# Laying the high and low halves of the weights among each other, element by element, in a two-layer encoder

## The chip, the cores and the metric

The kernel runs on one core of a Trainium2 chip. Its time is the device time of one execution in microseconds (us); smaller is better. A profiled execution gives the trace that is read here: for each engine (PE for matmuls, PEld for the weight loads of the same engine, DVE, ACT, POOL, and SP, which issues the transfers) the start and length of its instructions.

## The reference

The reference is a trunk of two layers over 256 tokens of width 2048, all in float32. Each layer has two parts, and each part adds its result to the running activations `x`:

```
h = rmsnorm(x, norm_mix[l]) * (1 + sc_a) + sh_a
qa, ka, va, qb, kb, vb, ga, gb = split_cols(h @ w_in[l])
ya = window_attention(qa, ka, va, sink_a[l]) @ w_proj_a[l]
yb = neighbourhood_attention(qb, kb, vb, rel_bias_b[l]) @ w_proj_b[l]
merged = sigmoid(ga) * ya + sigmoid(gb) * yb
x = x + gt_a * (merged @ w_out[l])
h = rmsnorm(x, norm_ffn[l]) * (1 + sc_m) + sh_m
u = depthwise_conv(h @ w_up[l], conv_w[l], conv_b[l])
g, v = split(u)
x = x + gt_m * ((silu(g) * v) @ w_down[l])
```

The shifts, scales and gates (`sh`, `sc`, `gt`) come from a small vector `c` through a matrix `ada_w` of 2048 x 12288 per layer. The weights of one layer are 232 x 16 blocks of 128 x 128 floats, each used once per execution.

## The kernel before

**Split products.** Matmuls run in the type fp32r, which keeps fewer bits than float32. To get float32 accuracy the kernel splits each operand into a high half (the value rounded to fp32r) and a low half (what is left) and adds three products: high weight by high activation, high weight by low activation, low weight by high activation.

**Weights.** The weights come in units of 16 blocks, 1 MB each, in the order in which TensorE uses them. `unit` (line 216) transfers a unit into a tile `w` of the pool `raw` (four buffers) and splits it in two halves of eight blocks. For each of these it takes a tile `hl` (a pool of four buffers, 8 KB per partition each); ACT writes the rounded values into its first 4 KB (line 225, a cast), and DVE subtracts them from the raw values and writes the rest into its last 4 KB (line 226). So there are 928 casts and 928 subtractions of 128 x 1024 elements. Before the change all the high values of eight blocks lie one after another, and then all the low ones.

**Feature stages.** In all products but q, k and v the weight block is the stationary operand: `feature_run` (line 229) loads 128 columns of `hl` and streams an activation tile past them. In the first layer's mixer (`joint`) each block gives three matmuls of 256 columns (lines 239, 240, 241), each with a weight load of its own. Everywhere else a block gives one matmul of 512 columns with the high weights (high and low activation side by side; lines 248 and 253) and one of 256 columns with the low weights (line 250). The first are called wide here, all those of 256 columns narrow. They run in groups of up to eight blocks: for the first half of a sum over 16 blocks the wide ones and then the narrow ones, for the second half the narrow ones and then the wide ones.

**Token stages.** For q, k and v (`tokens`, lines 337 to 339) the roles are swapped: an activation block is stationary, and 512 columns of `hl` (four blocks) stream past it.

**What the stages read.** The streamed activations are the tiles `h` and `merged` (one buffer of the pool `h`), `oA` and `oB` (the outputs of the attention) and `act` (in the shared places `o`, `a`, `b0`, `b1`, `y0` to `y2`). In the built program `hl`, `h` and `merged` begin at a byte offset in the partition that leaves 32 when divided by 128; the places of `act`, `oB` and most of `oA` leave 96.

**Order.** The program's order on each engine comes from the order of the Python statements and a scheduler. The background work (attention heads, the products with `ada_w` on DVE at line 162) is paced by unit. SP issues all transfers of weights; ACT and DVE each run a single queue that holds the splitting of the weights and the evacuation of finished sums.

Of the kernel before, what the change touches and what calls it, by code (L numbers as in the profile page):

```python
# [9 lines left out]
F32 = mybir.dt.float32  # L10
F32R = mybir.dt.float32r
AF = mybir.ActivationFunctionType
ALU = mybir.AluOpType
AX = mybir.AxisListType

P = 128
L = 2
# [16 lines left out]
GATE_A, GATE_B = 4608, 6656  # L34
# [27 lines left out]
ATT = [1.288, 0.4]  # L62
ATT_B = [0.21, 0.21]

ADA_ORDER = [[p * KC + k for k in range(KC) for p in ps] for ps in ((0, 1), (2,), (3, 4), (5,))]
ADA_ORDER = [i for part in ADA_ORDER for i in part]


def block_stream(l):

    seq = []
    for part in K_PARTS[l]:
        for g in QKV_GROUPS:
            for kc in part:
                seq += [("w_in", kc, g // P + j) for j in range(4)]
        for mo in range(KC):
            seq += [("w_in", kc, GATE_A // P + mo) for kc in part]
    for mo in range(KC):
        seq += [("w_proj_a", kc, mo) for kc in range(HA)]
    for mo in range(KC):  # L80
        seq += [("w_in", kc, GATE_B // P + mo) for kc in range(KC)]
    for mo in range(KC):
        seq += [("w_proj_b", kc, mo) for kc in range(HB)]
    for mos in OUT_TURNS:
        seq += [("w_out", kc, mo) for kc in range(KC) for mo in mos]
    for gi, chunks in enumerate(FF_GROUPS):
        cols = [c + h * FC for c in chunks for h in range(2)]
        if gi == 0:
            for kc in range(KC):
                seq += [("w_up", kc, m) for m in cols[:4]]  # L90
            cols = cols[4:]
        for m in cols:
            seq += [("w_up", kc, m) for kc in range(KC)]
        for mos in OUT_TURNS:
            seq += [("w_down", kc, mo) for kc in chunks for mo in mos]
    return seq


UB = 16
NU = len(block_stream(0)) // UB  # L100
NA = len(ADA_ORDER)


@with_exitstack
def encoder(ctx: ExitStack, tc: tile.TileContext, a: dict, out: bass.AP):
    nc = tc.nc
# [4 lines left out]
    hlp = pool("hl", 4)  # L111
# [40 lines left out]
    def ada(l):  # L152
# [5 lines left out]
        mods[l], amods[l] = mod, amod  # L158
        for n, i in enumerate(ADA_ORDER):
            raw = rawp.tile([P, D], F32, name=f"aw{l}_{n}", tag="raw")  # L160
# [54 lines left out]

    def unit(l, u):

        raw = rawp.tile([P, UB * P], F32, name=f"w{l}_{u}", tag="raw")
        nc.sync.dma_start(raw[:], a["ws"][l, u])
        halves = []  # L220
        for j in range(2):
            n = UB * P // 2
            hl = hlp.tile([P, 2, n], F32R, name=f"hl{l}_{u}_{j}", tag="hl")
            r = raw[:, j * n : (j + 1) * n]
            nc.scalar.copy(hl[:, 0], r)  # L225
            nc.vector.tensor_tensor(out=hl[:, 1], in0=r, in1=hl[:, 0].bitcast(F32), op=ALU.subtract)  # L226
            halves.append(hl)
        return halves

    def feature_run(run, joint):  # L230

        wide, narrow = [], []
        for ps, hl, j, act, first, last in run:
            hi, lo = hl[:, 0, j * P : (j + 1) * P], hl[:, 1, j * P : (j + 1) * P]
            out = ps[:].rearrange("p (a s) -> p a s", a=2)
            if joint:
                nc.tensor.matmul(out[:, 0], hi, act[:, 0], start=first, stop=False)  # L239
                nc.tensor.matmul(out[:, 0], hi, act[:, 1], start=False, stop=False)  # L240
                nc.tensor.matmul(out[:, 0], lo, act[:, 0], start=False, stop=last)  # L241
                continue
            wide.append((out, hi, act, first, last))
            narrow.append((out[:, 0], lo, act[:, 0]))
        begins = any(w[3] for w in wide)
        for o, w, act, first, last in wide:
            if begins and not last:
                nc.tensor.matmul(o, w, act, start=first, stop=False)  # L248
        for o, w, act in narrow:
            nc.tensor.matmul(o, w, act, start=False, stop=False)  # L250
        for o, w, act, first, last in wide:
            if last or not begins:
                nc.tensor.matmul(o, w, act, start=False, stop=last)  # L253

    class Stream:
# [16 lines left out]
        def prefetch(self, n):  # L272

            for _ in range(n):
                self.ahead.append(unit(self.l, self.u + len(self.ahead)))
# [13 lines left out]
        def next_block(self):  # L289
            if self.at == UB:  # L290
                if self.ahead:
                    self.halves = self.ahead.popleft()
                else:
                    with self.held():
                        self.halves = unit(self.l, self.u)
                self.u, self.at = self.u + 1, 0
            j = self.at
            self.at += 1
            return self.halves[j // 8], j % 8

        def features(self, acts, evacs, late=None, joint=False):

            pss = [mm.tile([P, 512], F32, name=f"ps{self.l}_{self.u}_{self.at}_{m}", tag="mm") for m in range(len(evacs))]
            run = []
            for i, act in enumerate(acts):
                self.feed(i)
                for ps in pss:
                    hl, j = self.next_block()
                    run.append((ps, hl, j, act, i == 0, i == len(acts) - 1))
                    ends = i == len(acts) - 1 and ps is pss[-1]  # L310
                    if j == 7 or ends or self.near(late, i, acts, ps, pss):
                        feature_run(run, joint)
                        run = []
                        if late and i == len(acts) - LATE - 1:
                            late()
                    if self.at == UB:
                        self.tick()
            for ps, evac in zip(pss, evacs):
                evac(ps)
# [6 lines left out]
        def tokens(self, h, kcs):  # L326

            pss = [mm.tile([P, 512], F32, name=f"ps{self.l}_{self.u}_t{t}", tag="mm") for t in range(2)]
            for kc in kcs:
                self.feed(kc)  # L330
                for _ in range(4):
                    hl, j = self.next_block()
                j -= 3
                hi, lo = hl[:, 0, j * P : (j + 4) * P], hl[:, 1, j * P : (j + 4) * P]
                for t, ps in enumerate(pss):
                    xh, xl = (h[:, kc, i, t * P : (t + 1) * P] for i in range(2))
                    nc.tensor.matmul(ps[:], xh, hi, start=kc == kcs[0], stop=False)  # L337
                    nc.tensor.matmul(ps[:], xh, lo, start=False, stop=False)  # L338
                    nc.tensor.matmul(ps[:], xl, hi, start=False, stop=kc == kcs[-1])  # L339
                if self.at == UB:  # L340
                    self.tick()
            return pss
# [622 lines left out]
```

## Time and profile before

| What | Value |
|---|---|
| Time, median of 3 runs | 2773.54 us (2771.54 to 2773.58) |
| Profiled execution, its own time | 2775.14 us |
| Its span, first to last instruction | 2773.4 us |
| PE busy | 2715.0 us (98%), 15930 matmuls |
| PEld busy | 2398.7 us (86%), 15930 loads |
| DVE busy | 2214.0 us (80%) |
| ACT busy | 1450.3 us (52%) |
| Mean granted TensorE clock | 0.991 |
| DMA, mean | 252 GB/s |

[...] The pace is read from the starts: the time from one matmul's start to the next one's. Where the timeline merges several equal matmuls in one line, the pace is the line's length, less the length of one record, divided by the number of matmuls less one.

### The profile page before, as it was taken

The numbers are of one execution on the slowest core, as the hardware profiler recorded it, in microseconds if no ns is written. First come the engines' busy times: TensorE is split into PE (matmuls) and PEld (weight loads), VectorE is DVE, ScalarE is ACT, GpSimd is POOL, SyncE is SP. The second block draws the span as 40 slices with busy tenths as digits, with TensorE's granted clock in tenths as the row PEclk, the third lists the DMA queues.
The fourth block names the chain that finished last, engine by engine and source line by source line (L and its number), as shares of the span: only waits on it lengthen the run. The fifth ranks groups of instructions, "written<-read, shape, count | busy, mean of one in ns | idle before, by whom it ended". The sixth has DMA issues, their size and how long they took to land.

```text
span 2773.4 us, 39861 instructions
## 1 busy us (share of the span) xinstructions
PE 2715.0 (98%) x15930; PEld 2398.7 (86%) x15930; DVE 2214.0 (80%) x3163; ACT 1450.3 (52%) x2137; POOL 39.3 (1%) x24
## 2 busy tenths in 40 slices
PE   7899999999999999999999999999989999999999
PEld 5788799998888888888878888888878888888888
DVE  6998987897999888789976666768989767766775
ACT  5344684444654455355544567555455535544553
POOL 0000100000000000000000000000000000000000
PEclk9999999999999999999999999999999999999999
DMA  8887588896778766777756666665867655555553
GB/s 314 334 329 264 214 308 329 329 331 231 279 279 328 276 255 245 271 274 286 291 190 238 228 227 233 232 254 199 306 222 287 243 190 187 193 186 194 184 196 137
DMA packets 101852, 699.72 MB, mean 252 GB/s; under 512 B 12705, under 2 KB 15009, under 8 KB 17697
## 3 DMA queue, kind: packets, MB, share of 16 engines
q1 hardware_dynamic: 101666, 697.17, 68.2%
q8 instruction: 125, 2.05, 0.3%
q14 instruction: 61, 0.50, 0.1%
HBM read 695.03 MB, written 2.10 MB: 251 GB/s over the span
## 4 chain that ended last, share of the span: by engine, by line
PE 79%; issue 14%; DVE 4%; POOL 1%; ACT 1%; DMA 0%; POOLq 0%; SPq 0%; ACTq 0%; DVEq 0%
PE ps L253 20%; PE ps L250 18%; PE ps L248 15%; PE ps_t L338 4%; PE ps L240 4%; PE ps L239 4%; PE ps L241 4%; PE ps_t L339 4%; PE ps_t L337 4%; DVE aw L162 1%; DVE hl L226 1%; POOL qrs L390 1%; PE sc L485 1%; PE po L516 1%; ACT hl L225 0%
## 5 line engine op out<-in xcount | busy, mean ns | idle before, releaser
L226 DVE TENSOR_TENSOR hl<-w,hl 128x1024 fp32r<-128x1024 f32 x928 | 1131.3, 1223 | 307.6 <-ACT hl L225 300.8
L225 ACT CAST hl<-w 128x1024 fp32r<-128x1024 f32 x928 | 972.5, 1050 | 756.3 <-PE ps L253 174.5
L162 DVE CUSTOM_DVE_ANT_0 aw<-aw,cact,ab 128x2048 f32<-128x2048 f32 x192 | 450.7, 2347 | 25.5 <-DMA aw<-in_aw 25.1
L250 PEld LDWEIGHTS ps<-h,hl 128*128 128x128 f32 x3328 | 428.0, 191 | 16.9
L250 PE MATMUL ps<-h,hl 128*128 128x256 f32 x3328 | 432.9, 283 | 0.0
L253 PE MATMUL ps<-h,hl 128*128 128x512 f32 x1712 | 428.7, 392 | 0.0
L248 PE MATMUL ps<-h,hl 128*128 128x512 f32 x1616 | 406.4, 394 | 5.5 <-DVE cpad L347 4.5
L248 PEld LDWEIGHTS ps<-h,hl 128*128 128x128 f32 x1616 | 306.3, 190 | 70.8 <-DVE cpad L347 5.4
L253 PEld LDWEIGHTS ps<-h,hl 128*128 128x128 f32 x1712 | 307.9, 189 | 55.0
L346 ACT COPY r<-ps 128x256 f32<-128x256 f32 x240 | 88.9, 372 | 286.0 <-PE ps L253 286.0
L337 PE MATMUL ps_t<-hl,h 128*128 128x512 f32 x576 | 228.1, 401 | 7.5 <-ACT hl L225 7.0
L338 PE MATMUL ps_t<-hl,h 128*128 128x512 f32 x576 | 228.6, 397 | 4.7 <-DVE hl L226 4.7
L339 PE MATMUL ps_t<-hl,h 128*128 128x512 f32 x576 | 227.6, 396 | 0.9 <-DVE h L426 0.9
L826 DVE SCALAR_TENSOR_TENSOR u<-cpad,cw,u 128x256 f32<-128x256 f32 x352 | 168.7, 481 | 7.6 <-ACT u L824 3.2
L241 PE MATMUL ps<-h,hl 128*128 128x256 f32 x512 | 145.9, 285 | 0.0
L239 PE MATMUL ps<-h,hl 128*128 128x256 f32 x512 | 145.3, 284 | 0.0
L240 PE MATMUL ps<-h,hl 128*128 128x256 f32 x512 | 145.0, 283 | 0.0
L786 DVE SCALAR_TENSOR_TENSOR x<-ps,mod,x 128x256 f32<-128x256 f32 x237 | 111.5, 481 | 40.5 <-PE ps L253 30.4
L337 PEld LDWEIGHTS ps_t<-hl,h 128*128 128x128 f32 x576 | 109.8, 191 | 31.1 <-ACT hl L225 7.6
L338 PEld LDWEIGHTS ps_t<-hl,h 128*128 128x128 f32 x576 | 110.0, 191 | 30.8 <-DVE hl L226 8.1
L339 PEld LDWEIGHTS ps_t<-hl,h 128*128 128x128 f32 x576 | 109.9, 191 | 24.3 <-DVE h L426 1.4
L347 DVE TENSOR_TENSOR cpad<-ps,r 128x256 f32<-128x256 f32 x176 | 74.4, 424 | 63.2 <-ACT r L346 63.0
(202 smaller groups left out, 3610.4 us busy)
## 6 DMA issues: line engine op xcount, KB each, us to landing
w<-in_ws SPq DMA_DIRECT2D x464, 1024.0 KB, 4.9
aw<-in_aw SPq DMA_DIRECT2D x192, 1024.0 KB, 4.9
bias<-in_bias SPq DMA_DIRECT2D x16, 256.0 KB, 4.4
x<-in_xT SPq DMA_DIRECT2D x4, 512.0 KB, 5.6
out<-x SPq DMA_DIRECT2D x16, 128.0 KB, 1.8
cw<-in_cw SPq DMA_DIRECT2D x2, 176.0 KB, 4.0
maskA<-in_maskA SPq DMA_DIRECT2D x1, 256.0 KB, 5.3
ab<-in_ab SPq DMA_DIRECT2D x2, 48.0 KB, 7.1
```

The costliest lines, as they stand in the source:

```text
L162: nc.vector.tensor_tensor_reduce(out=raw[:], in0=raw[:], in1=cact[:], scale=1.0, scalar=ab[:, i : i + 1], op0=ALU.mult, op1=ALU.add, accum ...
L225: nc.scalar.copy(hl[:, 0], r)
L226: nc.vector.tensor_tensor(out=hl[:, 1], in0=r, in1=hl[:, 0].bitcast(F32), op=ALU.subtract)
L239: nc.tensor.matmul(out[:, 0], hi, act[:, 0], start=first, stop=False)
L240: nc.tensor.matmul(out[:, 0], hi, act[:, 1], start=False, stop=False)
L241: nc.tensor.matmul(out[:, 0], lo, act[:, 0], start=False, stop=last)
L248: nc.tensor.matmul(o, w, act, start=first, stop=False)
L250: nc.tensor.matmul(o, w, act, start=False, stop=False)
L253: nc.tensor.matmul(o, w, act, start=False, stop=last)
L337: nc.tensor.matmul(ps[:], xh, hi, start=kc == kcs[0], stop=False)
L338: nc.tensor.matmul(ps[:], xh, lo, start=False, stop=False)
L339: nc.tensor.matmul(ps[:], xl, hi, start=False, stop=kc == kcs[-1])
```

## The change

In three of every four units of a layer's weight stream (numbers 0, 1 and 2 of each four), unless the unit holds a block of q, k or v, the high and low values of `hl` no longer lie in two runs of 1024: value 0's high half comes first, then its low half, then value 1's high half, and so on. Tiles, sizes, buffers, transfers, instructions, their order on every engine and all waits are the same; only the addresses that ACT writes, DVE reads and writes and the weight load reads go in steps of two elements there. In the built program 584 of the 928 casts and of the 928 subtractions are of this kind, and the loads of 6144 narrow and 3936 wide matmuls.

```diff
+MESH = [True, True, True, False]
...
-NU = len(block_stream(0)) // UB
+STREAMS = [block_stream(l) for l in range(L)]
+NU = len(STREAMS[0]) // UB
...
     def unit(l, u):
         raw = rawp.tile([P, UB * P], F32, name=f"w{l}_{u}", tag="raw")
         nc.sync.dma_start(raw[:], a["ws"][l, u])
         halves = []
+        mesh = MESH[u % len(MESH)] and not any(m == "w_in" and mo < GATE_A // P for m, _, mo in STREAMS[l][u * UB : (u + 1) * UB])
         for j in range(2):
             n = UB * P // 2
-            hl = hlp.tile([P, 2, n], F32R, name=f"hl{l}_{u}_{j}", tag="hl")
+            hl = hlp.tile([P, 2 * n], F32R, name=f"hl{l}_{u}_{j}", tag="hl")
             r = raw[:, j * n : (j + 1) * n]
-            nc.scalar.copy(hl[:, 0], r)
-            nc.vector.tensor_tensor(out=hl[:, 1], in0=r, in1=hl[:, 0].bitcast(F32), op=ALU.subtract)
-            halves.append(hl)
+            both = hl[:].rearrange("p (n a) -> p a n" if mesh else "p (a n) -> p a n", a=2)
+            nc.scalar.copy(both[:, 0], r)
+            nc.vector.tensor_tensor(out=both[:, 1], in0=r, in1=both[:, 0].bitcast(F32), op=ALU.subtract)
+            halves.append(lambda a, j, n=1, both=both: both[:, a, j * P : (j + n) * P])
         return halves
...
-            hi, lo = hl[:, 0, j * P : (j + 1) * P], hl[:, 1, j * P : (j + 1) * P]
+            hi, lo = hl(0, j), hl(1, j)
...
-                hi, lo = hl[:, 0, j * P : (j + 4) * P], hl[:, 1, j * P : (j + 4) * P]
+                hi, lo = hl(0, j, 4), hl(1, j, 4)
```

## The prediction

> **What bounds the kernel now.** I read the page first: engine shares, then the groups. The columns of a group are line, engine, operation, output and inputs, count, then busy time, mean length of one, idle time before and who ended it.
>
> ```profile
> PE 2715.0 (98%) x15930; PEld 2398.7 (86%) x15930; DVE 2214.0 (80%) x3163; ACT 1450.3 (52%) x2137; POOL 39.3 (1%) x24
> ...
> L226 DVE TENSOR_TENSOR hl<-w,hl 128x1024 fp32r<-128x1024 f32 x928 | 1131.3, 1223 | 307.6 <-ACT hl L225 300.8
> L225 ACT CAST hl<-w 128x1024 fp32r<-128x1024 f32 x928 | 972.5, 1050 | 756.3 <-PE ps L253 174.5
> ```
>
> TensorE hardly ever waits, so the span is its pace; the splitting is beside it, and ACT waits for buffers that TensorE frees. The timeline of PE alone, at four places, shows the pace (start us, length us of the merged line):
>
> ```profile
> 469.79 0.28 PE L239 MATMUL ps<-h,hl 128*128 128x256 f32 x1
> 469.91 0.28 PE L240 MATMUL ps<-h,hl 128*128 128x256 f32 x1
> 470.03 0.28 PE L241 MATMUL ps<-h,hl 128*128 128x256 f32 x1
> ...
> 539.83 0.28 PE L239 MATMUL ps<-oB,hl 128*128 128x256 f32 x1
> 539.94 0.28 PE L240 MATMUL ps<-oB,hl 128*128 128x256 f32 x1
> 540.06 0.28 PE L241 MATMUL ps<-oB,hl 128*128 128x256 f32 x1
> ...
> 1101.15 2.08 PE L250 MATMUL ps<-h,hl 128*128 128x256 f32 x16
> 1103.06 2.00 PE L253 MATMUL ps<-h,hl 128*128 128x512 f32 x8
> ...
> 1119.69 2.02 PE L253 MATMUL ps<-act_y,hl 128*128 128x512 f32 x8
> 1121.55 2.03 PE L248 MATMUL ps<-act_b,hl 128*128 128x512 f32 x8
> ...
> 1900.70 1.07 PE L250 MATMUL ps<-oB,hl 128*128 128x256 f32 x8
> ...
> 2168.80 1.98 PE L248 MATMUL ps<-h,hl 128*128 128x512 f32 x8
> ```
>
> Narrow matmuls that stream `h` start 0.120 us apart: (2.08 - 0.283) / 15, and the first three lines. Those that stream `oB` start (1.07 - 0.276) / 7 = 0.113 us apart. Wide ones on `h` need (1.98 - 0.394) / 7 = 0.227 (line 248) or (2.00 - 0.393) / 7 = 0.230 (line 253), on `act` 0.232 to 0.234. Shape, type, engine queue and neighbours are the same; what differs is where the streamed tile lies against the weights. The view by tile says it in one column (min/median/max ns of one):
>
> ```profile
> L250 PE MATMUL ps<-h,hl x3328: 274/283/415, 674.2 to 2695.1; 128*128 128x256 f32 x196
> L250 PE MATMUL ps<-act_b,hl x384: 276/276/282, 1106.8 to 2549.9; 128*128 128x256 f32 x192
> ```
>
> So a weight load and the matmul that it runs beside disturb each other by an amount that hangs on their addresses, and the change alters the load's addresses. The weight load is the shorter leash for narrow matmuls: transposes with only 128 streamed columns start 0.109 us apart, (0.60 - 0.273) / 3, so 0.109 is what a load of 128 columns needs by itself:
>
> ```profile
> 1700.12 0.60 PE L510 MATMUL tp<-ident,p 128*128 128x128 f32 x4
> 1700.56 1.03 PE L485 MATMUL sc<-packB 128*128 128x256 f32 x4
> ```
>
> **The change, part by part.** (1) Instructions, order, waits, buffers, transfers: none added or moved, on SP, POOL or elsewhere; cost zero, with nothing that needs cover. (2) ACT's cast writes, and DVE's subtraction reads and writes, in steps of two elements, 584 times each. No row here has such a step. Upper bound: half rate. For DVE the part of 1.223 us that grows with length comes from the 256-element L347 at 0.424: (1223 - 424) / 768 = 1.04 ns per element, so at most +1.07 us each, 622 us of DVE work; for ACT, from L346 at 0.372, (1050 - 372) / 768 = 0.88 ns, at most +0.90 us, 528 us. Lower bound: nothing, since one element per step of the engine is already all that 1.04 ns allows; a gain has no row. I take zero, because DVE's rate is the same whether it streams 256, 1024 or 2048 elements (L162: 2347), which says the arithmetic sets it and not the memory. If ACT's bound came true, 1450 + 528 = 1978 us would still fit; DVE's is a rival below.
>
> The Trainium skill, SBUF — State Buffer, on cachelines under "Door 1", says that memory lines are 16 bytes and that two hits on a line keep full rate; every second fp32 is exactly two hits. By that the strided cast, subtraction and load cost nothing by themselves. No run here shows it.
>
> (3) The weight load reads 128 elements over 1024 bytes instead of 512. The streamed operand moves through 1024 bytes in the 0.113 us of a narrow matmul, and the load's 0.109 us now covers 1024 bytes as well: the two walk at the same speed, where before the stream overtook the load. Two walkers at one speed either never meet or, once one has been held up, stop meeting; walkers at different speeds meet again and again. So I expect the disturbed paces to fall to the least disturbed that this trace has, 0.113 narrow and 0.227 wide. Of the 6144 narrow matmuls with changed loads 4352 stream `h` or `merged`: 4352 x (0.120 - 0.1134) = 28.7 us; the other 1792 are within about 0.001 of it: 2 us. Of the 3936 wide ones, 2720 stream `h` or `merged`; half of these are at line 253: 1360 x 0.003 = 4 us; the 1216 on `act`, `oA`, `oB` give 1216 x 0.006 = 7 us. Sum 42 us.
>
> Bounds of (3): downwards, if nothing disturbs any more: narrow 0.109 (L510) and wide 0.216, L485's pace of (1.03 - 0.380) / 3 rounded: with mean paces of 0.118 and 0.230 that is 6144 x 0.009 + 3936 x 0.014 = 110 us less. Upwards, moderate: a load over twice as many bytes collides twice as often; the step from 0.113 to 0.120 is then paid once more, 6144 x 0.0067 = 41 us, and the wide ones pay their excess over 0.227 once more, 4 us at line 253 on `h` and 9 us on `act`: together 54 us more. Upwards, extreme: the load takes a step of two at half rate, 0.218 us, and narrow matmuls follow it: 6144 x 0.100 = 614 us; wide ones at 0.230 still cover it. I take the 42 us, as the rows nearest to it exist in the kernel itself, at the same shapes.
>
> (4) What then comes next: at 42 us less, DVE's 2214 us and the DMA's 252 GB/s mean stay below the new span; in the tightest stretch of the changed part (680 to 800 us, DVE busy 111.76 of 120) a gain of about 2% still fits. I allow 3 us for this and for the first loads after a switch. The profiled execution took 2775.14 us, 1.6 above the median: 2775.1 - 42 + 3 = 2736, against the median 2735.
>
> **The rivals.** *Nothing moves.* The pace might be set by the stream alone, with 0.120 against 0.113 due to where the streamed tile lies and not to the load. Against: the two tiles differ only in offset; for: wide matmuls pay less on `h` and more on `act`, so no tile is simply the bad one. It gives 2774. The Trainium skill says so outright, in TensorE: Matmul & The Clock Gate, the weight-load step under "Step-by-step: what each phase is for": the engine has two independent read ports, and loading the next weights takes nothing from the running matmul. The trace disagrees so far as a row can: 276 against 283 ns for the same form.
>
> *Slower by collisions*, at the weight load: the moderate upper bound above, 54 us, 2828. For it: twice the bytes per load. Against: equal speeds. It decides as soon as narrow matmuls on `h` pass 0.120.
>
> *Slower by DVE*, at line 226: at half rate DVE's load rises by about 0.29 us per us (622 us over the 2093 us that lie behind 400 us and outside the second layer's q, k and v, 1420 to 1700); added to its share by stretch (0.79 at 400 to 500, 0.90, 0.78, 0.93 at 680 to 800, 0.88, 0.81, 0.87, then 0.77, 0.80, 0.72, 0.66) it passes 1 in all but the last, which sums to about 190 us: 2965. It decides where the subtraction passes about 1.47 us (the 8 us free at 680 to 800 over 33 changed tiles).
>
> *Slower by a half-rate load*: 614 us, 3388; it decides from a load longer than the 0.120 us of the narrow pace.
>
> *Undisturbed altogether*: 110 us less, 2664.
>
> **How the numbers follow.** Forecast (paces fall to the best of this trace, 2715 to 2765): 0.52. Undisturbed or nearly (2664 to 2715): 0.08. Nothing: 0.08. Collisions (2780 to 2840): 0.17. DVE: 0.08. Half-rate load: 0.07. So faster by over 0.2% (5.5 us, about what a measurement of this kernel can tell from no change) 0.60, within it 0.08, slower 0.32. The forecast's own range is 2715 to 2765. The whole range takes in half of the undisturbed case, all collisions and the mildest of DVE: 2695 to 2850, leaving out the half-rate load, most of DVE's case and the extreme gain, about 0.17.
>
> **What would show it.** In the profile after: the narrow matmuls of line 250 on `h` at a median of 276 instead of 283 ns and 16 of them in about 1.98 us; unchanged units still at 2.08; the two forms of the cast and the subtraction at the same length, 1.05 and 1.22 us; PE's share still 98%. Wrong, if the subtraction with the step exceeds 1.47 us and PE waits for `hl`, or if narrow matmuls in changed units start more than 0.120 us apart.

## The result, and the profile after

The changed kernel is slower: 2801.98 us against 2772.54 us, a ratio of 1.0106 (95% interval 1.0089 to 1.0124). The page of its profiled execution, whose span is 2799.9 us, 26.5 more than before:

```profile
PE 2740.1 (98%) x15930; PEld 2436.4 (87%) x15930; DVE 2217.7 (79%) x3163; ACT 1494.9 (53%) x2137; POOL 39.3 (1%) x24
...
L233 ACT CAST hl<-w 128x1024 fp32r<-128x1024 f32 x928 | 1023.8, 1105 | 784.3 <-PE ps L261 169.1
L234 DVE TENSOR_TENSOR hl<-w,hl 128x1024 fp32r<-128x1024 f32 x928 | 1131.8, 1223 | 334.9 <-ACT hl L233 330.6
```

(Lines are eight further down from the helpers on: 225, 226, 248, 250, 253 are now 233, 234, 256, 258, 261.) TensorE is as full as before, 98%; so it did not wait for anybody, it got slower. DVE's subtraction did not change by a nanosecond. ACT's cast did: 344 of the 928 are unchanged at 1.050 us, so the 584 others take (1023.8 - 344 x 1.050) / 584 = 1.135 us. PEld, the weight loads, is up by 37.7 us: in the changed units the median load takes 195 ns beside narrow matmuls and 196 beside wide ones, where it took 192 and 188.

The view by source line of the narrow matmuls (min/median/max ns), and the timeline of PE in a stretch that streams `h` and one that streams `oB`:

```profile
L258 PE MATMUL ps<-h,hl x3328: 277/283/416, 675.9 to 2720.8; 128*128 128x256 f32 x196
L258 PE MATMUL ps<-act_b,hl x384: 276/282/288, 1114.9 to 2573.3; 128*128 128x256 f32 x192
```

```profile
1084.74 2.03 PE L256 MATMUL ps<-h,hl 128*128 128x512 f32 x8
1086.61 2.08 PE L258 MATMUL ps<-h,hl 128*128 128x256 f32 x16
1088.52 2.05 PE L261 MATMUL ps<-h,hl 128*128 128x512 f32 x8
...
1907.10 1.12 PE L258 MATMUL ps<-oB,hl 128*128 128x256 f32 x8
```

The narrow matmuls on `h` were to fall from 283 to 276 ns; they stayed, 16 of them still taking 2.08 us. Instead those on `act` and `oB` rose to the slow pace: (1.12 - 0.282) / 7 = 0.120 us against 0.113. And the wide ones on `h` went from 0.227 and 0.230 to (2.03 - 0.400) / 7 = 0.233 at line 256 and (2.05 - 0.396) / 7 = 0.236 at line 261. (Paces are taken from the starts because records overlap: a narrow one on `h` is 0.283 us long, and the next starts after 0.120.)

Adding up the times from each matmul's start to the next one's, by what is streamed (rows where TensorE stood for over 0.4 us left out), gives the whole bill, in us:

| Matmuls | before | after | difference |
|---|---|---|---|
| narrow on `h`, `merged` | 709.7 | 710.8 | +1.1 |
| narrow on `act`, `oA`, `oB` | 286.6 | 296.9 | +10.3 |
| wide on `h`, `merged` | 806.6 | 825.2 | +18.6 |
| wide on `act`, `oA`, `oB` | 380.0 | 377.8 | -2.2 |
| sum | | | +27.8 |

The span grew by 26.5 us; what the table leaves out (long waits, q, k and v, the attention) makes up the difference of about 1 us. What it leaves open is whether the loads read slower or the writes disturb them, and why the load at equal speed did not get out of the stream's way.

### The profile page after: what moved, and what is told of

Its sections match the earlier page's. It is cut to its first block, busy times and chain, and to the rows that moved or that the text cites. A ratio compares the mean times of both kernels' runs of the same rounds, so it can differ in the third digit from the quotient of the medians.

```text
span 2799.9 us, 39861 instructions
## 1 busy us (share of the span) xinstructions
PE 2740.1 (98%) x15930; PEld 2436.4 (87%) x15930; DVE 2217.7 (79%) x3163; ACT 1494.9 (53%) x2137; POOL 39.3 (1%) x24
## 3 DMA queue, kind: packets, MB, share of 16 engines
q8 instruction: 125, 2.05, 0.3%
## 4 chain that ended last, share of the span: by engine, by line
PE 79%; issue 14%; DVE 4%; POOL 1%; ACT 1%; DMA 1%; POOLq 0%; SPq 0%; ACTq 0%; DVEq 0%
PE ps L261 20%; PE ps L258 18%; PE ps L256 16%; PE ps_t L346 4%; PE ps L248 4%; PE ps L249 4%; PE ps L247 4%; PE ps_t L347 4%; PE ps_t L345 4%; DVE aw L166 1%; DVE hl L234 1%; POOL qrs L398 1%; PE po L524 1%; PE sc L493 1%; ACT hl L233 0%
## 5 line engine op out<-in xcount | busy, mean ns | idle before, releaser
L233 ACT CAST hl<-w 128x1024 fp32r<-128x1024 f32 x928 | 1023.8, 1105 | 784.3 <-PE ps L261 169.1
L258 PEld LDWEIGHTS ps<-h,hl 128*128 128x128 f32 x3328 | 430.7, 195 | 17.3
L261 PE MATMUL ps<-h,hl 128*128 128x512 f32 x1712 | 435.4, 396 | 0.0
L256 PE MATMUL ps<-h,hl 128*128 128x512 f32 x1616 | 416.9, 400 | 5.6 <-DVE cpad L355 4.7
L256 PEld LDWEIGHTS ps<-h,hl 128*128 128x128 f32 x1616 | 315.5, 196 | 72.3 <-DVE cpad L355 5.5
L261 PEld LDWEIGHTS ps<-h,hl 128*128 128x128 f32 x1712 | 316.9, 194 | 51.3
```

The costliest lines, as they stand in the source:

```text
L233: nc.scalar.copy(both[:, 0], r)
```

## The experiments

### Only the load reads in steps of two

```diff
-            both = hl[:].rearrange("p (n a) -> p a n" if mesh else "p (a n) -> p a n", a=2)
+            apart, among = hl[:].rearrange("p (a n) -> p a n", a=2), hl[:].rearrange("p (n a) -> p a n", a=2)
+            wr, rd = apart, among if mesh else apart
```

ACT and DVE then write to `wr`, and the matmuls load from `rd`.

> ACT and DVE write the high and low halves apart, as before the change; only the weight load reads in steps of two elements, in the same units as the changed kernel (so it multiplies by wrong weights: high and low values mixed; the work is otherwise the same). Load theory (the step of the load makes the load and the stream beside it disturb each other more): about the whole loss, 2800 us, with wide matmuls on h 0.235 us apart instead of 0.229 and narrow ones on oB and act 0.120 instead of 0.114. Write theory (ACT's cast, which went from 1.05 to 1.14 us in the changed units, or the writes' own disturbance of TensorE's reads): about the time before, 2773 us, with the paces of before.

2801.69 us, ratio 1.0097 (1.0083 to 1.0111): the whole loss. By starts, each of the four groups of the table lies within about 1 us of the changed kernel. The wide matmuls on `h` at line 262 (261 in the changed kernel) have the same busy time as there, 435.4 us, and the cast is back at its old length:

```profile
L234 ACT CAST hl<-w 128x1024 fp32r<-128x1024 f32 x928 | 973.9, 1051 | 794.4 <-issue 180.9 <-PE ps L262 178.4 <-PE ps L259 156.5
L262 PE MATMUL ps<-h,hl 128*128 128x512 f32 x1712 | 435.4, 396 | 0.0
```

### Only the writes go in steps of two

```diff
-            wr, rd = apart, among if mesh else apart
+            wr, rd = among if mesh else apart, apart
```

> The reverse: ACT and DVE write the halves among each other in the changed units, the weight load reads in steps of one (wrong weights again). Load theory: 2773 us, the paces of before, with ACT's cast still at 1.14 us. Write theory: 2800 us. If both parts cost something, the two kernels share the 28 us.

2776.61 us, ratio 1.0008 (0.9999 to 1.0017): no loss that can be told from none.

```profile
L234 ACT CAST hl<-w 128x1024 fp32r<-128x1024 f32 x928 | 1021.6, 1103 | 735.2 <-PE ps L262 162.7 <-PE ps L259 134.9 <-ACT u L833 114.9
L262 PE MATMUL ps<-h,hl 128*128 128x512 f32 x1712 | 428.7, 392 | 0.0
```

ACT's longer cast is there (its mean is 1103 ns) and costs nothing, since ACT is busy about half of the time; TensorE's row is that of the kernel before, 428.7, and by starts each of the four groups lies within 1 us of it. So the step of the load, and not that of the writes, is the cause.

### Every unit, the fourth ones too

```diff
-MESH = [True, True, True, False]
+MESH = [True]
```

> The halves among each other in every unit without q, k, v, the fourth ones too. Load theory: the loss grows with the number of changed loads, by about 4/3, so 28 x 4/3 = 37 us over the kernel before, 2810 us. A theory by which the switching between the two layouts is what costs: less than the changed kernel, below 2800 us.

2810.39 us, ratio 1.0133 (1.0117 to 1.0148), 36.4 us over the kernel before. The loss goes by the number of strided loads, as forecast; it is not the switching between layouts that costs, and leaving out every fourth unit only makes the loss smaller.

### Steps of four

```diff
+            if mesh:
+                four = hl[:].rearrange("p (n b) -> p b n", b=4)
+                halves.append(lambda a, j, n=1, four=four: four[:, a + 2 * (j // 4), (j % 4) * P : (j % 4 + n) * P])
...
```

(in the changed units; the others read as before)

> Written apart as before the change; the weight load of the same units reads in steps of four elements, one element of each 16 bytes (wrong weights again). If the disturbance grows with the bytes that a load runs over (512, 1024, now 2048): a few per cent, some 2830 to 2860 us, narrow ones near 0.125 us. If a load needs two hits in 16 bytes to keep its rate, as the Trainium skill says in SBUF — State Buffer (cachelines, under Door 1): the load takes about twice its 0.109 us, narrow matmuls start about 0.218 us apart, 2773 + 6144 x 0.100 = about 3390 us. If the step makes no difference beyond two: 2800 us.

3498.71 us, ratio 1.2614 (1.2597 to 1.2631). The median load beside narrow matmuls on `h` goes from 192 ns to 329, and the narrow matmuls follow it:

```profile
L262 PEld LDWEIGHTS ps<-h,hl x3328: 187/329/334, 917.4 to 3400.2; 128*128 128x128 f32 x196
...
1406.95 3.78 PE L262 MATMUL ps<-h,hl 128*128 128x256 f32 x16
```

(3.78 - 0.394) / 15 = 0.226 us. So a load in steps of four runs at about half rate, as was forecast for it; the wide matmuls also lose, which was not, and which is part of the 110 us over the forecast: 0.243 us on `h` and 0.250 on `act` as a mean of the starts in changed units, against 0.229 and 0.232.

### The load by itself

Behind the end of the kernel before, rows of 40 equal matmuls with one changed thing each: 128 streamed columns (short), 256 (narrow) or 512 (wide), the load's step, and the byte at which the streamed tile begins (a 0, b 32, c 64, d 96 further).

```diff
+    def probe(name, n, step, off, times=40):
+        ps = mm.tile([P, 512], F32, name=name, tag="mm")
+        w = wf.rearrange("p (n b) -> p b n", b=step)[:, 0, :P]
+        for _ in range(times):
+            tc.keep_in_program_order(nc.tensor.matmul(ps[:, :n], w, hf[:, off : off + n], start=True, stop=True))
...
```

> The kernel before, with rows of 40 equal matmuls added behind its end (the results of these are not used): 128, 256 or 512 streamed columns of h, against a weight load from hl in steps of one, two or four elements, with the streamed tile begun 0, 32, 64 or 96 bytes further; then 512 columns streamed from hl itself in steps of one, two, four. Theory A (the load with two elements per 16 bytes is by itself slower): with 128 streamed columns, where the load sets the pace, step one gives 0.109 us, step two clearly more (0.115 or above), step four about 0.22. Theory B (load and stream disturb each other, the load alone is as fast as before): step two still gives 0.109 with 128 columns, and only 256 and 512 columns get slower. Under both, step one should be at 0.113 to 0.120 (256 columns) and 0.227 to 0.236 (512), by where the tile begins, and step two at 0.120 and 0.229 to 0.235.

The timeline merges each row of 40 in a line (start us, length us):

```profile
2767.38 4.58 PE L898 MATMUL short_one_a<-h,hl 128*128 128x128 f32 x40
2771.79 5.00 PE L898 MATMUL narrow_one_a<-h,hl 128*128 128x256 f32 x40
2776.63 9.26 PE L898 MATMUL wide_one_a<-h,hl 128*128 128x512 f32 x40
...
2804.23 4.58 PE L898 MATMUL short_one_c<-h,hl 128*128 128x128 f32 x40
2808.64 4.93 PE L898 MATMUL narrow_one_c<-h,hl 128*128 128x256 f32 x40
2813.41 9.33 PE L898 MATMUL wide_one_c<-h,hl 128*128 128x512 f32 x40
...
2841.18 4.81 PE L898 MATMUL short_two_a<-h,hl 128*128 128x128 f32 x40
2845.83 5.02 PE L898 MATMUL narrow_two_a<-h,hl 128*128 128x256 f32 x40
2850.68 9.49 PE L898 MATMUL wide_two_a<-h,hl 128*128 128x512 f32 x40
...
2888.48 9.49 PE L898 MATMUL wide_two_c<-h,hl 128*128 128x512 f32 x40
...
2916.68 9.37 PE L898 MATMUL short_four_a<-h,hl 128*128 128x128 f32 x40
...
3029.24 9.27 PE L909 MATMUL stream_one<-hl,h 128*128 128x512 f32 x40
3038.36 18.29 PE L909 MATMUL stream_two<-hl,h 128*128 128x512 f32 x40
```

With 128 columns the stream is short, and the load sets the pace. From start to start, with the first few of a row left out, that is a mean of 0.1116 us in steps of one, at every offset, 0.1177 to 0.1191 in steps of two, and 0.234 in steps of four. Theory A holds: a load of every second element is slower by 6 to 7.5 ns already beside a short stream. (No row has a load with no stream at all beside it.) Narrow matmuls need 0.118 to 0.120 us in steps of one, by offset, and 0.120 to 0.121 in steps of two; the 0.113 of the kernel, which both theories had for some offset, appears in none of these rows, and 0.120 is some 2 ns more than the strided load needs, which suggests that some disturbance is left on top of the slower load. Wide matmuls in steps of two need 0.2333 to 0.2336 us at all four offsets, where steps of one gave 0.2267 to 0.2333 by offset. So in these rows the new layout made the wide pace independent of where the tile begins, but at the bad end of the range. In the changed kernel itself that is not so: in its changed units wide matmuls start 0.235 us apart on `h` and 0.231 on `act`. The last two lines show why the change spares q, k and v: a *streamed* operand in steps of two takes twice as long, (18.29 - 0.63) / 39 = 0.453 us against 0.227.

### One kind of load at a time

The read-only kernel again, with the step of two for the low weights only, then for the high ones only:

```diff
-            halves.append(lambda a, j, n=1, rd=rd: rd[:, a, j * P : (j + n) * P])
+            halves.append(lambda a, j, n=1, rd=rd, apart=apart: (rd if a == 1 else apart)[:, a, j * P : (j + n) * P])
```

(`a == 0` for the high weights)

> Written apart; only the loads of the low weights read in steps of two, in the changed units (wrong weights). If each strided load costs for itself: narrow matmuls on act, oA, oB at 0.119 to 0.120 instead of 0.114 (about 9 us), on h no change; wide ones as before: about 2783 us. If it is the pair of high and low in the same bytes that costs: 2774 us.

2782.87 us, ratio 1.0034 (1.0021 to 1.0046). By starts, the narrow matmuls on `act`, `oA`, `oB` took 296.0 us against 286.6, and no other group moved by more than 1.0 us: this term stands alone, as forecast.

> Written apart; only the loads of the high weights read in steps of two (wrong weights). If each strided load costs for itself: wide matmuls on h at 0.234 instead of 0.2286 (about 18 us), those on act 1 to 2 us less, and two of three narrow ones on oB in the first layer 1 to 2 us more: about 2791 us. The losses of this run and of the one with low weights should add to the 28 us. If the pair costs: 2774 us.

2782.27 us, ratio 1.0034 (1.0022 to 1.0046), some 9 us less than forecast. The wide matmuls on `h` and `merged` took 816.8 us: 10.2 more than before, but 8.4 less than in the changed kernel. The timeline at about the same place:

```profile
1089.18 2.03 PE L257 MATMUL ps<-h,hl 128*128 128x512 f32 x8
1091.05 2.07 PE L259 MATMUL ps<-h,hl 128*128 128x256 f32 x16
1092.95 2.02 PE L262 MATMUL ps<-h,hl 128*128 128x512 f32 x8
```

The wide rows at line 262 (253 before) take 2.02 us here and 2.05 in the changed kernel, with the same strided loads of high weights in both. The two runs sum to 18.6 us of the 27.7 of the run with all loads strided; most of the rest appears in the wide matmuls on `h` only when the narrow ones between them are strided as well. What is carried from a row of narrow matmuls into the next row of wide ones stays open.

### Moving the streamed tile instead

The probe's step-one rows differ by offset, so a better offset might be had without touching the weights. First `h` and `merged` 64 bytes further, with the weights apart as before the change; the second pad moves all tiles behind them by 128:

```diff
     hlp = pool("hl", 4)
+    nc.vector.memset(pool("pad0", 1).tile([P, 16], F32, name="pad0")[:], 0.0)
     hp = pool("h", 1)
+    nc.vector.memset(pool("pad1", 1).tile([P, 16], F32, name="pad1")[:], 0.0)
```

> The kernel before with h and merged begun 64 bytes further, so that they lie against hl as act and oB do; nothing else changes. If the offset sets the paces: the 2352 narrow matmuls of the first layer's mixer that stream h or merged go from 0.120 to 0.114 us, about 14 us less; elsewhere on h narrow ones gain 0.006 and wide ones lose 0.004, about 6 us less together: some 2753 us. If the place of the tile and not its offset mattered: 2773 us.

2765.24 us, ratio 0.9964 (0.9952 to 0.9977): faster, by half of what was forecast. Two things had been left out. In q, k and v the same two tiles meet with roles swapped, and there the pace rose from 0.228 or 0.229 to 0.234 or 0.235 us as a mean of all. Two lines from the kernel before (337) and two from this run (339), in each case six matmuls apart, show 1.36 us and 1.40:

```profile
1500.35 0.39 PE L337 MATMUL ps_t<-hl,h 128*128 128x512 f32 x1
...
1501.71 0.39 PE L337 MATMUL ps_t<-hl,h 128*128 128x512 f32 x1
...
1500.79 0.39 PE L339 MATMUL ps_t<-hl,h 128*128 128x512 f32 x1
...
1502.19 0.39 PE L339 MATMUL ps_t<-hl,h 128*128 128x512 f32 x1
```

There `hl` is streamed and stayed in its place; only the tile that is loaded had moved. So the place of the streamed tile alone does not set the pace: it is the two tiles together. And `oB` lost, though it only moved by 128 bytes, with the second pad (line 241 here is 239 before):

```profile
L241 PE MATMUL ps<-oB,hl x128: 280/280/280, 525.8 to 570.7; 128*128 128x256 f32 x128
```

That was 276 before. The changed kernel with the same pads:

> The changed kernel with the same 64 bytes. In the changed kernel narrow matmuls need 0.120 us at either offset, and wide ones 0.235 at h's and 0.231 at act's. So h gains only on the wide ones: 2650 x 0.004 = 11 us, and the unchanged units gain a few: about 2788 us. If the disturbance at step two does not hang on the offset: 2800 us.

2803.67 us, ratio 1.0104 (1.0088 to 1.0119): nothing gained. The wide matmuls on the feed-forward `h` did fall, from 0.2339 to 0.2323 us, but q, k and v (0.228 and 0.229 to 0.234 and 0.235), the narrow ones on the first layer's `oB` (0.1184 to 0.1207) and the wide ones on `act` (0.231 to 0.233 in changed units) took it back. So at a step of two, too, the paces hang on the places of the tiles, by about 2 ns.

Then all of `h` and `merged` 192 bytes further, and the rest by 256, so that it keeps its remainder of 256:

```diff
+    OFF = {n: 192 for n in ("h0_0", "merged0", "h0_1", "h1_0", "h1_1", "merged1")}
+
+    def htile(name):
+        o = OFF.get(name, 0) // 4
+        n = KC * 2 * S
+        t = hp.tile([P, n + 64], F32R, name=name, tag="h")
+        return t[:, o : o + n].rearrange("p (k a s) -> p k a s", k=KC, a=2)
...
-        h = hp.tile([P, KC, 2, S], F32R, name=f"h{l}_{w}", tag="h")
+        h = htile(f"h{l}_{w}")
```

(the same for `merged`)

> The kernel before with h and merged of both layers 192 bytes further. If the paces repeat every 128 bytes: the time of the run with 64 bytes, 2765 us. If they repeat every 256: as act and oB before, narrow 0.114 and wide 0.2328; narrow gains 1531 x 0.0065 + (1408 + 512 + 1408 + 766 + 287) x 0.0055 = 34 us, wide loses 3527 x 0.0042 = 15 us, q, k, v lose 1670 x 0.0065 = 11 us: about 2766 us as well, but with those paces in the rows.

2761.02 us, ratio 0.9957 (0.9944 to 0.9969). The paces on the second layer's feed-forward `h` are those of `act` before: narrow 0.1140, wide 0.2332. The same in a stretch of the first layer's:

```profile
1072.90 2.03 PE L256 MATMUL ps<-h,hl 128*128 128x512 f32 x8
1074.77 1.98 PE L258 MATMUL ps<-h,hl 128*128 128x256 f32 x16
```

Nearly all such rows take 1.98 us here, where with 64 bytes they alternate between 1.98 and 2.04 or 2.05. So 64 and 192 bytes are not the same, and the paces do not repeat every 128. q, k and v lose less than at 64 bytes, 0.2295 to 0.231 us, or 3 us instead of 11. In the first layer's mixer, though, `h` and `merged` came only to 0.1176 and 0.1179, and `oB`, which had only moved by 256, went from 0.1134 to 0.1178. These paces are from the slowest of the five executions, 2767.65 us; what made the others up to 9 us faster is not known, and so neither is why the median lies 5 us under the forecast.

### Each tile where its stage is fastest

The same helper, with `o` by tile: `h` and `merged` of the first layer's mixer 192 bytes further, `h` of both feed-forward parts and the second layer's `merged` 64, the second layer's mixer `h` as it was.

```diff
-    OFF = {n: 192 for n in ("h0_0", "merged0", "h0_1", "h1_0", "h1_1", "merged1")}
+    OFF = {"h0_0": 192, "merged0": 192, "h0_1": 64, "h1_1": 64, "merged1": 64}
```

> The kernel before (weights apart) with each streamed tile put where its own stage is fastest: the first layer's mixer h and merged 192 bytes further (the offset of oB, 0.113 us narrow), the second halves' h and the second layer's merged 64 bytes further (0.116 narrow, 0.229 wide in the run with h moved by 64), the second layer's mixer h as it is, since q, k and v lose there. Offset theory: h of the first mixer gains 1531 x 0.0065 = 10 us and its q, k, v lose 828 x 0.006 = 5 us; merged 5 us; h of both feed-forward parts 2 x 1400 x (0.0040 - 0.0008) = 9 us; merged of the second layer 1 us: together 20 us, about 2754 us. If only the offset by a remainder of 128 counted, the tiles at 192 would behave like those at 64: about 5 us less gain.

2753.98 us, ratio 0.9934 (0.9921 to 0.9947): 19 us under the kernel before and 48 under the changed one. The time is the forecast one, its terms are not quite: in the profiled execution, whose span of 2759.9 us is at the slow end of this version's runs (2750.77 to 2761.63 us in all), `h` of the first mixer gained 5 us of the 10 and `merged` 2 of the 5, q, k and v lost 1.4 of the 5, `oB` lost 1.7, and the feed-forward `h` gave 6.8 of the 9. The timeline in the stretch that streams the feed-forward `h`:

```profile
1071.42 2.05 PE L258 MATMUL ps<-h,hl 128*128 128x256 f32 x16
...
1075.15 2.00 PE L256 MATMUL ps<-h,hl 128*128 128x512 f32 x8
1076.98 1.98 PE L258 MATMUL ps<-h,hl 128*128 128x256 f32 x16
1078.80 1.99 PE L261 MATMUL ps<-h,hl 128*128 128x512 f32 x8
```

16 narrow ones take 1.98 or 2.05 us, row by row in turn, where they took 2.08; the wide ones take 1.99 to 2.00 at both lines, against 1.98 and 2.00. The weights lie apart, and the load reads in steps of one.

The last version answers the first mixer's 0.118: 448 bytes for its `h` and `merged`, and 512 for all that follows.

```diff
-    OFF = {"h0_0": 192, "merged0": 192, "h0_1": 64, "h1_1": 64, "merged1": 64}
+    OFF = {"h0_0": 448, "merged0": 448, "h0_1": 64, "h1_1": 64, "merged1": 64}
...
-        t = hp.tile([P, n + 64], F32R, name=name, tag="h")
+        t = hp.tile([P, n + 128], F32R, name=name, tag="h")
```

> In the last run but this one the first layer's mixer h and merged, 192 bytes further, came to 0.118 us narrow and not to 0.1134, and so did oB, which had only moved by 256 bytes. So this kernel puts those two tiles 448 bytes further (oB's own offset by a remainder of 512 in the kernel before) and moves all the other tiles by 512. If the paces of the first layer's narrow matmuls repeat every 512 bytes: oB back at 0.1134, merged at 0.1134 and h at 0.115 to 0.118, that is 384 x 0.0044 + 766 x 0.0045 + up to 1531 x 0.003 = 5 to 10 us below the 2754 us of the version before: 2744 to 2749 us. If the offset by 512 is not what decides: 2754 us, with oB still at 0.118.

The paces did as the period of 512 says: `oB` is back, by the view of its tile,

```profile
L247 PE MATMUL ps<-oB,hl x128: 276/276/276, 516.4 to 559.6; 128*128 128x256 f32 x128
```

where the version before had 281/281/281 in this row; `merged` starts 0.1143 us apart and `h` 0.1151. The profiled span is 2751.8 us, 8 less than that of the version before, which had its slowest execution profiled. But the time, 2755.38 us, ratio 0.9942 (0.9929 to 0.9955), is not the forecast 2744 to 2749; it is that of the version before, within the spread: executions of both versions range over 11 to 12 us (2752.78 to 2764.78 here), twice as far as those of the kernel before (2771.22 to 2776.37). What makes them spread is not known. Either version beats both kernels.

## Why the prediction was wrong

**Reading of the bound: right.** TensorE's pace is the span, before and after; and the pace of equal matmuls does hang on where the streamed tile lies against the weights. The runs with moved tiles show that with the instructions unchanged, and q, k and v show that it is not the streamed tile's place alone. The rival by which a load takes nothing from the stream is refuted: the strided high loads alone took wide matmuls on `h` from 0.2286 to 0.2315 us, though such a load, at 0.118 us, takes about half of a wide matmul's time. The Trainium skill says, in TensorE: Matmul & The Clock Gate, the weight-load step under "Step-by-step: what each phase is for", that loading the next weights takes no read bandwidth from the running matmul. These rows disagree in so far as the load is not free for the stream; which resource they share no run here shows.

**(1) Nothing added or moved: right.** The number of instructions on each engine is that of before.

**(2) ACT and DVE at zero cost: right in the sum, wrong in one size.** DVE's subtraction has the same 1.223 us; the cast grew by 0.085 us, within the bounds of 0 to 0.90, and lies beside other work (the run with writes alone). The Trainium skill, SBUF — State Buffer, on cachelines under "Door 1", says that two hits on a line of 16 bytes keep full rate. That held for DVE here. It did not hold for ACT (+8%), for the load (+6%), nor for a streamed operand (half rate); with one hit per line the load went from 0.112 to 0.234 us.

**(3) Paces fall to the best of the trace, 42 us: this step failed.** It took 0.109 us as what a load of 128 columns needs by itself (from line 510, which is float32), and kept it for a load of every second element. The probe, in fp32r, has 0.112 and 0.118. With that the narrow matmuls on `h` could not go to 0.113, as their loads take longer than that: the 28.7 us of gain came out as 1.1 us of loss, and the other narrow ones, which were to gain 2 us, lost 10.3, because most of them had been at 0.113 or 0.114 and now start 0.120 apart. (Not all had: those on `oA` in the first layer start 0.125 apart in the changed units before, and 0.129 after.) For the wide ones, whose loads are short enough in either layout, it was the picture of two walkers that failed. They did not stop meeting: in changed units the pace is 0.235 us on `h` and 0.231 on `act`, not 0.227. That turned 4 us of gain on `h` into 18.6 of loss, and 7 us of gain on `act` into 2.2. The starts along a row of eight on the second layer's `h` (line 253, now 261; mean of 93 rows) show it. Before, they are 233, 236, 228, 232, 231, 227, 227 and 227 ns apart: with the load at its old step the row comes to rest after five. After, they are 238, 233, 235, 238, 233, 235, 238 and 231 apart, and it never does. Why a strided load keeps meeting the stream, which is two thirds of the loss, stays open.

**(4) and the range.** What would come next was never reached. The time lies inside the range and the case of collisions, at about half its price: of the 54 us, 41 were for narrow matmuls paying 6.7 ns once more everywhere, and only those that were fast paid; 13 were for wide ones, which paid 16.4. (Of the 13, the 9 on `act` are priced above the 7 of gain there, though both are the same excess over 0.227.) Its mechanism, more collisions with twice the bytes, was not shown either: the probe puts most of the narrow part on a slower load, and for the wide part it is neither shown nor excluded. The lower bound of 0.216 us for wide ones was read from line 485, whose matmuls stream 256 columns of float32 and not 512 of fp32r; the fastest rows of the latter here come to rest at 0.227.

**Rivals by DVE and by a half-rate load** did not happen; the second is what steps of four do.

The error lies in choosing the middle. The trace had no strided load, and the bounds were set on both sides by rows, one of them of another type; the value between them came from a picture of two walkers that no row supported. The nearest sure reading was that narrow matmuls at 0.113 us have their load, 0.109 by line 510, close behind: a longer load soon shows there, and a gain is capped by it.

## What to carry to other kernels

Where a stationary tile is reloaded for every matmul of 256 columns, the load is close to being the pace (here 0.112 us of 0.113 to 0.120); keep its elements next to each other, and do not expect a wider stride to be free because another engine, here DVE, does not notice it. If equal matmuls run at different paces on different tiles, try the tiles' offsets first: a pad of two lines here gave 0.4%, and a place for each tile 0.6 to 0.7%, where a new weight layout lost 1.1%. Test a pad on every stage that reads the tile, as a second stage may want another offset.

## What was not expected of the hardware

- A load of 128 fp32r columns in steps of one, two and four elements paced short matmuls at 0.112, 0.118 and 0.234 us: between two and four elements lies a cliff, between one and two a small step.
- A streamed fp32r operand has its cliff already at two: 0.227, 0.453, 0.461 us for 512 columns in steps of one, two, four.
- The paces with contiguous loads hang on how the streamed tile and the weights lie to each other: on the feed-forward `h` narrow 0.120, 0.116, 0.114 and wide 0.229, 0.229, 0.233 us at 0, 64 and 192 bytes. In the rows of narrow matmuls alone (first mixer) 192 and 448 differ as well, 0.118 and 0.114 on `merged`, which fits a period of 512 bytes.
- ACT's cast of 1024 elements into every second element took 1.135 us instead of 1.050; DVE's subtraction that reads and writes such a tile took 1.223 in both.
